# An encoder trunk on one core: tokens in column order for both mixers, and mixer B's probabilities turned in a band by 12 GpSimd copies in both layers

## The chip, the cores and the metric

One Trainium2 chip; the kernel runs on one of its NeuronCores. The engines that matter are TensorE (PE, with its weight loads shown apart as PEld), VectorE (DVE), ScalarE (ACT), GpSimd (POOL) and SyncE (SP), which here issues every DMA. The metric is the device time of one execution in microseconds (us), lower is better.

## The reference

Two layers, each a mixer sub-layer and a ConvFFN sub-layer, on 256 tokens of 2048 features; c is one conditioning vector. Cut to what matters:

```python
GRID_W, NA_KH, NA_KW, WIN = 64, 8, 16, 128     # SEQ 256: a grid of 4 rows of 64 tokens
for l in range(2):
    sh_a, sc_a, gt_a, sh_m, sc_m, gt_m = split(silu(c) @ ada_w[l] + ada_b[l], 6)
    h = rmsnorm(x, norm_mix[l]) * (1 + sc_a) + sh_a
    qa, ka, va, qb, kb, vb, ga, gb = split_cols(h @ w_in[l])
    ya = window_attention(rope(norm(qa)), rope(norm(ka)), va, sink_a[l]) @ w_proj_a[l]   # |i-j| <= 128, 8 heads
    yb = neighbourhood_attention(norm(qb), norm(kb), vb, rel_bias_b[l]) @ w_proj_b[l]    # 8 heads
    x = x + gt_a * ((sigmoid(ga) * ya + sigmoid(gb) * yb) @ w_out[l])
    h = rmsnorm(x, norm_ffn[l]) * (1 + sc_m) + sh_m
    g, v = split(depthwise_conv(h @ w_up[l], conv_w[l], conv_b[l]), 2)
    x = x + gt_m * ((silu(g) * v) @ w_down[l])
```

In mixer B a token sees the keys of all four grid rows in a window of 16 grid columns around its own column; the rest of a row of scores is masked.

## The kernel before

**Matrix work.** Activations lie with features on the 128 partitions and tokens along the free axis. Every float32 product with a big weight is made of three fp32r products of halves: weight and activation are each split into a rounded high part and the remainder (hi·hi, hi·lo, lo·hi). Weights stream from HBM in units of 16 blocks of 128x128 (1 MB, tile `w`); each half unit is cast on ACT into the high part of an `hl` tile (L326) and the remainder is made on DVE (L327). Four `hl` tiles and four raw tiles rotate, so a weight DMA, and behind it in SP's one queue all later DMAs, waits for a raw tile to come free. `feature_block` (L343 to L345) is the product for 128 output features of all 256 tokens; `tokens` (L406 to L408) is the q/k/v projection with tokens on the output partitions.

**Conditioning.** `ada` streams 96 tiles of 1 MB per layer (`aw`), each reduced by one DVE instruction (L233) into one column of `mod`; a plan by unit number says when.

**The mixer.** `normed` (L491 on) makes h: per 128 features a DVE instruction `ht` (L497), an ACT instruction (L500) and a DVE one (L501). The projection's groups of four heads pass through `qk_rows` (norms, rope, a turn to features on partitions) into the tiles `packA`, `packB`. Then heads run in a generator, `attention`: one call advances every live head by one stage and may start one more. Calls come from a pacer that ticks once per weight unit: 1.288 calls per tick in layer 0 until the last head of mixer A is done, then 0.36; 0.4 in layer 1. The stages of `attend` (L646 on) are:

1. scores on PE into PSUM `sc` (L651): one plain float32 product per 128 queries in layer 0 (two PE instructions each), three fp32r products in layer 1;
2. bias and row maximum on DVE (L654), exponent (L662) and scaling (L670) on ACT, in the tile `p`; in mixer B `p` holds the bias, loaded by a DMA, and then the scores;
3. the turn of the probabilities. In layer 0 four PE transposes per head into PSUM `tp` (L681). In layer 1 (`MOVED = [(0,0), (8,8)]`) one DVE transpose of 32x32 blocks into rows that are no longer needed (L304), then 16 GpSimd copies that put the blocks in place (L298), and one call of waiting;
4. the split into fp32r halves, `pT`, by an ACT cast (L418) and a DVE subtraction (L421); where the turn was made on DVE and GpSimd the cast is held in the program's order on ACT. `pT` has one buffer, so the next head's split waits until the products with v have read it;
5. six products with v (`po`, L689), and the output's split (L691, L692).

**The order of the work** on each engine comes from a list scheduler that runs when the program is built; an engine then takes its instructions strictly in that order, so a waiting instruction holds all that stands behind it. After the heads of layer 0 come: the projection of mixer A (`oA`, evacuated by `gated`, L434), the gate of mixer B, the merge (L1010 on: `gated` into a tile `m`, `ya` added in place (L1014), split), the output projection, the FFN.

**Constants.** `maskA` (256 KB) and the rope table `cs` are loaded by one DMA each, in `small` (L786 on) at the second of three passes over the q/k/v projection.

Of the kernel before, what the change touches and what calls it, by code (L numbers as in the profile page):

```python
# [15 lines left out]
P = 128  # L16
L = 2
D = 2048
S = 256
# [11 lines left out]
BLOCK = 32  # L31

# [57 lines left out]
MOVED = [(0,0), (8,8)]  # L90
# [51 lines left out]
def encoder(ctx: ExitStack, tc: tile.TileContext, a: dict, out: bass.AP):  # L142
# [45 lines left out]
    sp = pool("s", 1)  # L188

# [118 lines left out]

    def unit_steps(l, u, by_halves=False):
# [133 lines left out]
    class Squares:  # L443


        def __init__(self, name):
            self.acc = ev.tile([P, S], F32, name="sqa", tag="sqa", bufs=1)
            self.ps = ax.tile([P, 2, 2], F32, name=name, tag="ss", bufs=1)

        def add(self, mo):  # L450
            sq = self.acc if mo == 0 else ev.tile([P, S], F32, name="sq", tag="r", bufs=2)
            nc.scalar.activation(out=sq[:], in_=x[:, mo], func=AF.Square)
            if 0 < mo < KC - 1:
                nc.vector.tensor_tensor(out=self.acc[:], in0=self.acc[:], in1=sq[:], op=ALU.add)
            if mo == KC - 1:
                self.last = sq
# [34 lines left out]
    def normed(l, w, h, rbs):  # L491

        mod, amod = mods[l], amods[l]
        for kc in range(KC):
            t = ev.tile([P, S], F32, name="ht", tag="z")
            sh = mod[:, 3 * w * KC + kc : 3 * w * KC + kc + 1]
            nc.vector.scalar_tensor_tensor(  # L497
                out=t[:], in0=x[:, kc], scalar=amod[:, w, kc : kc + 1], in1=rbs[:], op0=ALU.mult, op1=ALU.mult
# [147 lines left out]
    def attend(q, k, v, p, mask, scale, sink, o, rows=None):  # L646

        sc = ax.tile([P, 2, S], F32, name="sc", tag="ax")
        for t in range(2):
            for i, j in by(q):  # L650
                nc.tensor.matmul(sc[:, t], q[i][:, t * P : (t + 1) * P], k[j], start=i + j == 0, stop=(i, j) == by(q)[-1])  # L651
        m = sm.tile([P, 2], F32, name="m", tag="m")
        for t in range(2):
            nc.vector.tensor_tensor_reduce(  # L654
                out=p[:, t], in0=sc[:, t], in1=mask[:, t], scale=scale, scalar=-3.0e38 if sink is None else sink,
                op0=ALU.add, op1=ALU.max, accum_out=m[:, t : t + 1],
            )
# [3 lines left out]
        for t in range(2):  # L661
            nc.scalar.activation(out=p[:, t], in_=p[:, t], func=AF.Exp, bias=nm[:, t : t + 1], accum_out=den[:, t : t + 1])  # L662
# [6 lines left out]
        for t in range(2):  # L669
            nc.scalar.activation(out=p[:, t], in_=p[:, t], func=AF.Copy, scale=ri[:, t : t + 1])  # L670
# [11 lines left out]
        pT = at.tile([P, 2, 2, S], F32R, name="pT", tag="pT", bufs=1)  # L682
        split(pT, tp[:], held=rows is not None)
# [101 lines left out]

    def small(l):  # L786

        if l == 0:
            tables.extend((load(a["maskA"], [P, 2, S], "maskA"), load(a["cs"], [P, 2, 2, HALF], "cs")))
# [18 lines left out]
    for l in range(L):  # L808
# [17 lines left out]
        if l:  # L826


            def bare_gate(mo):
                def evac(ps):  # L830
                    z, sh = bare.level(ps, 0.5)
                    half_tanh(ya[:, mo], z[:], bias=sh[:, :1])
# [17 lines left out]
        def head_a(i):  # L850
# [18 lines left out]
            def rows():  # L869
# [3 lines left out]
                q, k, v, p, tables[0], SCALE, sink[:, i : i + 1], lambda: oA[i], rows if i < MOVED[l][0] else None  # L873
            )

        def head_b(hb):
# [3 lines left out]
            nc.sync.dma_start(p[:], a["bias"][l, hb])  # L880
# [4 lines left out]
                q, k, lambda: in_halves(v[:, :, i * HEAD : (i + 1) * HEAD], f"vB{l}_{hb}", "vh", True), p, p, 1.0, None,  # L885
                lambda: oB_of(hb), (lambda: b[:, i : 9 + i : 8]) if hb < MOVED[l][1] else None,
            )

# [37 lines left out]
        for pi, (groups, gates) in enumerate(parts):  # L926
            last = pi == len(parts) - 1
            for g, part in enumerate(groups):
                have_h(part)
                pss = st.tokens(h, part)  # L930
                if pi == max(0, len(parts) - 2) and g == 0:
# [77 lines left out]
        for mo in range(KC):  # L1009

            def merge(ps):
                z = ev.tile([P, S], F32, name="m", tag="z")
                gated(z[:], gb[mo], ps)
                nc.vector.tensor_tensor(out=z[:], in0=z[:], in1=ya[:, mo], op=ALU.add)  # L1014
                split(merged[mo], z[:], 0.5)
# [188 lines left out]
```

## Time and profile before

| | us |
|---|---|
| median of 3 runs | 2655.18 (2653.85 to 2655.35) |
| the profiled execution: its own time | 2661.45 |
| its span in the trace | 2659.6 |
| PE busy (99%), weight loads busy (96%) | 2643.3, 2557.9 |
| DVE busy (80%) | 2121.0 |
| ACT busy (53%) | 1408.9 |
| GpSimd busy (9%) | 228.2 |

The granted TensorE clock is 1.00 throughout. The profiled execution lies 6.3 us above the median of the runs. A row of a group gives line, engine, operation, tile written <- tiles read, shapes and count, then busy time, the mean of one, and the idle time before them. A row by time gives start, duration, engine, line, and in brackets how long the engine was idle before it and on whom it waited. PE durations are latencies (about 277 ns for a 256-column product); the spacing of starts, about 113 to 117 ns, is what one costs in a stream.

### The profile page before, as it was taken

Reading aid. Unit: us, or ns where it says so; the run is one execution under the profiler, and the core shown is the slowest. Engines: PE = TensorE matmul, PEld = TensorE weight load, DVE = VectorE, ACT = ScalarE, POOL = GpSimd, SP = SyncE. Lnnn points to the kernel's source line nnn. Section 1 sums busy time; section 2 is a strip of 40 time slices with the busy share of each in tenths; the row PEclk is TensorE's granted clock in tenths of the full one; section 3 lists DMA queues with packets and bytes.
Section 4 is the critical chain, followed back from the end, with each engine's and each line's share of the span. In section 5 each row is a group of like instructions: output and inputs, shape, how many; then the busy total and the mean of one; then the engine's idle time right before and its main releaser. Section 6 shows DMA issues by size and latency. Waiting matters only on the chain.

```text
span 2659.6 us, 51014 instructions
## 1 busy us (share of the span) xinstructions
PE 2643.3 (99%) x21164; PEld 2557.9 (96%) x21164; DVE 2121.0 (80%) x2979; ACT 1408.9 (53%) x2280; POOL 228.2 (9%) x345
## 2 busy tenths in 40 slices
PE   9999999999999999999999999999999999999999
PEld 7888899999999999999998889999999999999999
DVE  8898998997987888788886778868888866655664
ACT  5445865456643555355554666654565445544553
POOL 0001100000000000000002558520000000000000
PEclk9999999999999999999999999999999999999999
DMA  9987779885777777877766666666747765555554
GB/s 371 349 329 292 267 294 356 316 339 184 295 272 289 284 287 285 306 296 285 283 221 253 249 234 232 253 258 257 283 178 287 297 252 191 192 196 194 196 191 143
DMA packets 102042, 700.42 MB, mean 263 GB/s; under 512 B 12721, under 2 KB 15025, under 8 KB 17969
## 3 DMA queue, kind: packets, MB, share of 16 engines
q1 hardware_dynamic: 101810, 697.17, 70.8%
q8 instruction: 165, 2.70, 0.4%
q14 instruction: 67, 0.55, 0.1%
HBM read 695.03 MB, written 2.10 MB: 262 GB/s over the span
## 4 chain that ended last, share of the span: by engine, by line
PE 86%; DMA 5%; DVE 5%; issue 2%; ACT 1%; POOL 0%; SPq 0%; DVEq 0%; ACTq 0%
PE ps L343 24%; PE ps L345 24%; PE ps L344 24%; DMA aw<-in_aw 4%; PE ps_t L408 4%; PE ps_t L407 4%; PE ps_t L406 4%; DVE hl L327 2%; DVE aw L233 1%; PE sc L651 1%; ACT hl L326 1%; PE po L689 1%; DMA w<-in_ws 1%; DVE u L1049 0%; POOL qrs L472 0%
## 5 line engine op out<-in xcount | busy, mean ns | idle before, releaser
L327 DVE TENSOR_TENSOR hl<-w,hl 128x1024 fp32r<-128x1024 f32 x928 | 1129.8, 1224 | 298.0 <-ACT hl L326 294.7
L326 ACT CAST hl<-w 128x1024 fp32r<-128x1024 f32 x928 | 969.8, 1049 | 719.7 <-PE ps L345 501.4
L343 PE MATMUL ps<-h,hl 128*128 128x256 f32 x3328 | 922.4, 277 | 1.3 <-DVE ya L970 0.6
L344 PE MATMUL ps<-h,hl 128*128 128x256 f32 x3328 | 919.6, 276 | 0.0
L345 PE MATMUL ps<-h,hl 128*128 128x256 f32 x3328 | 919.6, 277 | 0.0
L343 PEld LDWEIGHTS ps<-h,hl 128*128 128x128 f32 x3328 | 624.7, 188 | 2.4 <-DVE ya L970 0.8
L344 PEld LDWEIGHTS ps<-h,hl 128*128 128x128 f32 x3328 | 625.3, 188 | 0.4 <-DVE h L501 0.2
L345 PEld LDWEIGHTS ps<-h,hl 128*128 128x128 f32 x3328 | 624.4, 188 | 0.0
L233 DVE CUSTOM_DVE_ANT_0 aw<-aw,cact,ab 128x2048 f32<-128x2048 f32 x189 | 443.8, 2349 | 92.5 <-DMA aw<-in_aw 91.7
L406 PE MATMUL ps_t<-hl,h 128*128 128x512 f32 x576 | 223.0, 392 | 2.7 <-ACT h L500 2.0
L407 PE MATMUL ps_t<-hl,h 128*128 128x512 f32 x576 | 225.0, 391 | 0.3
L408 PE MATMUL ps_t<-hl,h 128*128 128x512 f32 x576 | 224.3, 390 | 0.0
L1049 DVE SCALAR_TENSOR_TENSOR u<-ps,cw,u 128x255 f32<-128x255 f32 x304 | 146.0, 480 | 62.0 <-ACT u L1047 58.1
L1047 ACT ACTIVATE u<-ps,cw 128x256 f32<-128x256 f32 x152 | 85.7, 564 | 155.4 <-PE ps L345 155.2
L343 PE MATMUL ps<-act_o,hl 128*128 128x256 f32 x512 | 142.0, 278 | 2.7 <-DVE u L1049 2.6
L345 PE MATMUL ps<-act_o,hl 128*128 128x256 f32 x512 | 142.1, 278 | 1.3 <-DVE hl L327 1.3
L344 PE MATMUL ps<-act_o,hl 128*128 128x256 f32 x512 | 142.0, 277 | 0.0
L345 PE MATMUL ps<-merged,hl 128*128 128x256 f32 x512 | 141.5, 277 | 0.0
L344 PE MATMUL ps<-merged,hl 128*128 128x256 f32 x512 | 141.5, 276 | 0.0
L343 PE MATMUL ps<-merged,hl 128*128 128x256 f32 x512 | 141.5, 277 | 0.0
L406 PEld LDWEIGHTS ps_t<-hl,h 128*128 128x128 f32 x576 | 107.9, 188 | 26.1 <-ACT h L500 3.0
L407 PEld LDWEIGHTS ps_t<-hl,h 128*128 128x128 f32 x576 | 108.1, 188 | 23.9 <-DVE hl L327 1.9
(244 smaller groups left out, 4800.3 us busy)
## 6 DMA issues: line engine op xcount, KB each, us to landing
w<-in_ws SPq DMA_DIRECT2D x463, 1024.0 KB, 4.9
aw<-in_aw SPq DMA_DIRECT2D x189, 1024.0 KB, 6.3
p<-in_bias SPq DMA_DIRECT2D x16, 256.0 KB, 4.5
x<-in_xT SPq DMA_DIRECT2D x4, 512.0 KB, 5.5
aw_o<-in_aw SPq DMA_DIRECT2D x2, 1024.0 KB, 12.4
out<-x SPq DMA_DIRECT2D x16, 128.0 KB, 3.2
w<-in_ws SPq DMA_DIRECT2D x2, 512.0 KB, 11.8
aw_b<-in_aw SPq DMA_DIRECT2D x1, 1024.0 KB, 18.1
```

What stands on the lines that cost most here:

```text
L233: nc.vector.tensor_tensor_reduce(out=raw[:], in0=raw[:], in1=cact[:], scale=1.0, scalar=ab[:, i : i + 1], op0=ALU.mult, op1=ALU.add, accum ...
L326: nc.scalar.copy(hl[:, 0], r)
L327: nc.vector.tensor_tensor(out=hl[:, 1], in0=r, in1=hl[:, 0].bitcast(F32), op=ALU.subtract)
L343: nc.tensor.matmul(out, hi, act[0], start=first, stop=False)
L344: nc.tensor.matmul(ps[:, :S], hi, act[1], start=False, stop=False)
L345: nc.tensor.matmul(out, lo, act[0], start=False, stop=last)
L406: nc.tensor.matmul(ps[:], xh, hi, start=kc == kcs[0], stop=False)
L407: nc.tensor.matmul(ps[:], xh, lo, start=False, stop=False)
L408: nc.tensor.matmul(ps[:], xl, hi, start=False, stop=kc == kcs[-1])
L651: nc.tensor.matmul(sc[:, t], q[i][:, t * P : (t + 1) * P], k[j], start=i + j == 0, stop=(i, j) == by(q)[-1])
L1047: nc.scalar.activation(out=u, in_=ps, func=AF.Identity, scale=w[:, 1:2], bias=w[:, 3:4])
L1049: nc.vector.scalar_tensor_tensor(out=u[:, to], in0=ps[:, of], scalar=w[:, j : j + 1], in1=u[:, to], op0=ALU.mult, op1=ALU.add)
```

## The change

**Token order.** A layer's mixer now works on tokens in column order: the four tokens of a grid column stand next to each other. `normed` writes `ht` in that order (runs of one element with a step of four), the bias, `maskA` and `cs` are loaded by `load_tokens` in 4 DMAs instead of 1 (8 for `cs`, whose two halves go apart), `maskA`'s columns are reordered by two GpSimd copies, the gate of layer 1 that is made from unnormalised x is written in the new order, and the merge writes the sum into a second tile, `m2`, back in the old order. `load_tables` is called in the first pass over the q/k/v projection, after its fourth group, ahead of where `small` loaded the tables.

**The band.** In column order 128 queries see 160 neighbouring keys (`NEAR`). For mixer B, in both layers, scores, mask, exponent, scaling and split work on 160 columns instead of 256, and the scores go into the two rows of q and k that the head has used up (`b[:, i:9+i:8]` of `packB`) instead of into `p`. The products with v keep 256 columns; the part of `pT` outside the band (two pieces of 96 columns per half) is set to zero once per layer by GpSimd.

**The turn.** `turned_near` takes the place of the four PE transposes in layer 0 and of DVE transpose and 16 copies in layer 1: a DVE transpose of the band into a tile of its own, `turned`, and 12 GpSimd copies back, 10 of 2x32 elements per partition on 32 partitions and 2 of 32. Its split is `split_near`, with the cast held on ACT. `MOVED = [0, 8]` keeps mixer A as it was: PE transposes in layer 0, DVE and 16 copies in layer 1. `WINDOWS_FROM = [0, 0]` turns all eight heads of mixer B in both layers.

**Tiles.** The two rotating square tiles of `Squares` (tag r) become one tile of the same total size, which `turned` shares by turns.

```diff
-MOVED = [(0,0), (8,8)]
+MOVED = [0, 8]
+WINDOWS_FROM = [0, 0]
...
+    def near(t):
+        return sheared(t, 0, S - NEAR, NEAR)
+    def load_tokens(dst, src):
+        rows = src.rearrange("(q w c) h f -> w q c h f", q=GRID_H // 2, w=2)
+        for w in range(2):
+            for q in range(GRID_H // 2):
+                nc.sync.dma_start(dst[q::2, w], rows[w, q])
...
+    def turned_near(p):
+        turned = ev.tile([P, 2, S], F32, name="turned", tag="r", bufs=1)[:]
+        nc.vector.transpose(out=near(turned), in_=near(p))
+        for a in range(P // BLOCK):
+            for d in (-1, 0, 1):
...
+                nc.gpsimd.tensor_copy(out=to, in_=of)
...
+    def split_near(dst, src, held):
+        high, low = near(dst[:, 0]), near(dst[:, 1])
+        copied = nc.scalar.copy(high, near(src))
+        if held:
+            tc.keep_in_program_order(copied)
+        nc.vector.tensor_tensor(out=low, in0=near(src), in1=high.bitcast(F32), op=ALU.subtract)
...
+            to, of, roots = (t[:], x[:, kc], rbs[:]) if w else (columns_by_row(t[:]), by_rows(x[:, kc]), by_rows(rbs[:]))
             nc.vector.scalar_tensor_tensor(
-                out=t[:], in0=x[:, kc], scalar=amod[:, w, kc : kc + 1], in1=rbs[:], op0=ALU.mult, op1=ALU.mult
+                out=to, in0=of, scalar=amod[:, w, kc : kc + 1], in1=roots, op0=ALU.mult, op1=ALU.mult
             )
...
-                nc.tensor.matmul(sc[:, t], q[i][:, t * P : (t + 1) * P], k[j], start=i + j == 0, stop=(i, j) == by(q)[-1])
+                nc.tensor.matmul(
+                    sc[:, t, :n], q[i][:, t * P : (t + 1) * P], k[j][:, part(t)], start=i + j == 0, stop=(i, j) == by(q)[-1]
+                )
...
+            to, of, add = p[:, t, part(t)], sc[:, t, :n], mask[:, t]
+            if window:
+                first = part(t).start // GRID_H
+                to, of = by_columns(to), by_columns(of)
+                add = rows_by_column(add)[:, first : first + n // GRID_H]
...
-            turned_blocks(p[:], rows(), 2)
-            for _ in range(STEPS[sink is None]):
+            if window:
+                turned_near(p)
+            else:
+                turned_blocks(p, rows(), 2)
+            for _ in range(STEPS[window]):
                 yield
...
-            tables.extend((load(a["maskA"], [P, 2, S], "maskA"), load(a["cs"], [P, 2, 2, HALF], "cs")))
+    def load_tables():
+        seen = at.tile([P, 2, S], F32, name="seen", tag="p")
+        load_tokens(seen[:], a["maskA"])
...
-            nc.sync.dma_start(p[:], a["bias"][l, hb])
+            load_tokens(p[:], a["bias"][l, hb])
...
-                nc.vector.tensor_tensor(out=z[:], in0=z[:], in1=ya[:, mo], op=ALU.add)
-                split(merged[mo], z[:], 0.5)
+                both = ev.tile([P, S], F32, name="m2", tag="z")
+                nc.vector.tensor_tensor(
+                    out=rows_by_column(both[:]), in0=by_columns(z[:]), in1=by_columns(ya[:, mo]), op=ALU.add
+                )
+                split(merged[mo], both[:], 0.5)
```

**How it moves instructions, at two places.** The first is the start of mixer B in layer 0, where the heads still come at 1.288 calls per tick. On DVE, from the second evacuation of mixer A's projection (`ya0`) on, before:

```order
L434 SCALAR_TENSOR_TENSOR ya0_222<-ya0_222,ps0_53_16_0_3417 128x256
L327 TENSOR_TENSOR hl0_54_0_3517<-w0_54_3515,hl0_54_0_3517 128x1024
L233 ISA aw0_45_3636,mod0_172<-aw0_45_3636,cact_100,ab0_173 128x2048
L233 ISA mod0_172 128x1
L421 TENSOR_TENSOR pT_3207<-tp_3202,pT_3207 128x512
L654 ISA p_3191,m_3216<-sc_3213,p_3191 128x256
```

and in the changed kernel at the same place (`packB0_0` holds the first head's probabilities, `hl0_54` and `hl0_55` are weight units):

```order
L377 TENSOR_TENSOR hl0_54_0_3558<-w0_54_3556,hl0_54_0_3558 128x1024
L347 STREAM_TRANSPOSE turned_3221<-packB0_0_224 128x2x160
L492 SCALAR_TENSOR_TENSOR ya0_222<-ya0_222,ps0_53_16_0_3446 128x256
L727 ISA packB0_0_224,m_3238<-sc_3235,p_3207 128x160
L727 ISA m_3238 128x1
L727 ISA packB0_0_224,m_3238<-sc_3235,p_3207 128x160
L727 ISA m_3238 128x1
L377 TENSOR_TENSOR hl0_54_1_3561<-w0_54_3556,hl0_54_1_3561 128x1024
L732 TENSOR_SCALAR nm_3241<-m_3238 128x2
L484 TENSOR_TENSOR pTB0_3324<-packB0_0_224,pTB0_3324 128x2x160
L492 SCALAR_TENSOR_TENSOR ya0_222<-ya0_222,ps0_54_8_0_3480 128x256
L377 TENSOR_TENSOR hl0_55_0_3621<-w0_55_3619,hl0_55_0_3621 128x1024
```

Between the transpose and the head's split (`pTB0`) now stand the second head's two mask instructions, half a weight unit and three short ones. The rest of unit 54 and unit 55 stand behind the split. On ACT the same head's cast is followed by the casts of the next units:

```order
L376 CAST hl0_54_1_3561<-w0_54_3556 128x1024
L685 ACTIVATE packB0_1_225<-qtp_3436,gains0_1005 128x4x128
L481 CAST pTB0_3324<-packB0_0_224 128x2x160
L376 CAST hl0_55_0_3621<-w0_55_3619 128x1024
L736 ACTIVATE packB0_0_224,den_3243<-packB0_0_224,nm_3241 128x160 x2
L376 CAST hl0_55_1_3624<-w0_55_3619 128x1024
```

so that a late copy holds back unit 55 on both engines.

The second place is SP's queue at the start. Before:

```order
L315 DMA w0_3_335<-in_ws 128x2048
L232 DMA aw0_7_371<-in_aw 128x2048
L315 DMA w0_4_383<-in_ws 128x2048
L232 DMA aw0_8_415<-in_aw 128x2048
L315 DMA w0_5_422<-in_ws 128x2048
```

and now:

```order
L365 DMA w0_3_335<-in_ws 128x2048
L223 DMA seen_349<-in_maskA 64x256 x4
L223 DMA cs_357<-in_cs 64x1x16 x8
L267 DMA aw0_7_388<-in_aw 128x2048
L365 DMA w0_4_400<-in_ws 128x2048
```

Twelve small DMAs moved ahead of the tile `aw0_7`; before, `maskA` and `cs` stood behind unit 15.

More of the change, by code (lines that the diff above doesn't have):

```diff
@@ L31 @@
 BLOCK = 32
+GRID_H = S // GRID_W
+NEAR = P + BLOCK
 QKV_GROUPS = [1024, 0, 512, 2560, 3584, 1536, 3072, 4096, 2048]
@@ L784, in encoder @@
     tables = []
+    def load_tables():
+        seen = at.tile([P, 2, S], F32, name="seen", tag="p")
+        load_tokens(seen[:], a["maskA"])
+        mask = const.tile([P, 2, S], F32, name="maskA")
+        for t in range(2):
+            nc.gpsimd.tensor_copy(out=by_columns(mask[:, t]), in_=rows_by_column(seen[:, t]))
+        cs = const.tile([P, 2, 2, HALF], F32, name="cs")
+        for f in range(2):
+            load_tokens(cs[:, f], a["cs"][:, f])
+        tables.extend((mask, cs))
     def small(l):
-        if l == 0:
-            tables.extend((load(a["maskA"], [P, 2, S], "maskA"), load(a["cs"], [P, 2, 2, HALF], "cs")))
         cs = tables[1]
```

66 lines of the change are left out of this document (53 added, 13 removed).

## The prediction

> **What bounds the kernel now.** I read the page's first lines and the chain that ended last, then the stretches which the change touches.
>
> ```profile
> span 2659.6 us, 51014 instructions
> PE 2643.3 (99%) x21164; PEld 2557.9 (96%) x21164; DVE 2121.0 (80%) x2979; ACT 1408.9 (53%) x2280; POOL 228.2 (9%) x345
> PE 86%; DMA 5%; DVE 5%; issue 2%; ACT 1%; POOL 0%; SPq 0%; DVEq 0%; ACTq 0%
> ```
>
> PE has work nearly all the time and carries 86% of the chain. What leaves PE's stream can therefore shorten the span, unless another engine stands right behind it. The view by stretches (per engine: busy time and instructions; then granted clock, DMA share, GB/s) says where one does: mixer B of layer 0 begins (340 to 376), goes on beside the projections (to 470), layer 0's merge (492 to 540), mixer B of layer 1 (1620 to 1680).
>
> ```profile
> 340.00:376.00 36.00, 36.00 (x288) 34.37 (x287) 34.45 (x69) 23.92 (x49) 0.00 (x0) 1.00 0.78 290
> 376.00:470.00 94.00, 94.00 (x813) 93.59 (x811) 85.09 (x118) 47.98 (x84) 0.00 (x0) 1.00 0.95 354
> 492.00:540.00 48.00, 48.00 (x422) 48.00 (x422) 47.49 (x81) 25.57 (x44) 0.00 (x0) 1.00 0.81 299
> 1620.00:1680.00 60.00, 60.00 (x529) 60.00 (x528) 51.32 (x78) 35.61 (x65) 48.48 (x78) 1.00 0.66 246
> ```
>
> In layer 0 PE and DVE are both full: DVE has 4% to spare at first, 1% in the merge, and from 376 on the DMAs are at 0.95. In layer 1 PE alone is full. So time taken from PE counts fully only while DVE is not made later.
>
> **What leaves PE.** The chain shows one head of mixer B in layer 0 (transposes, scores) and one head's scores in layer 1; the fourth row and its follower show products of one column.
>
> ```profile
> 375.79 0.44 PE tp L681 x4
> 376.23 0.86 PE sc L651 x4
> 1500.15 0.71 PE sc L651 x6
> 1934.65 0.50 PE L461 MATMUL ssm<-mean,sq 128*128 128x1 f32 x4
> 1935.01 0.36 PE L343 MATMUL ps<-bare_a,hl 128*128 128x258 f32 x1
> ```
>
> Transposes: 0.44 us a head, 8 heads, **-3.5 us**. Scores of layer 0: 0.86/4 = 215 ns an instruction at 256 columns; at 160 columns 134 ns in proportion. That is above the floor which the one-column products show (four start within 0.36 us, 90 ns each, with a weight load each), so 4 x 81 ns x 8 heads = **-2.6 us**. Together 6.1 us that PE certainly doesn't do.
>
> Scores of layer 1 are 48 fp32r products, 0.71/6 = 118 ns each at 256 columns. No fp32r product of fewer than 256 columns is in the trace. From below 90 ns bounds it (the one-column products): -1.3 us. From above the plain float32 rate, two instructions of 134 ns: 268 ns, +7.2 us. Nearest are fp32r products of 256 and 512 columns, whose cost goes with the columns, so I lean to the low end and take 105 ns: **-0.6 us**. The Trainium skill ("TensorE: Matmul & The Clock Gate", section "Back-to-back issue gap") gives N/2.4 + 2.5 ns for a warm product, whatever the type: 69 ns here by estimate, by which this term would be -2.4 us; the 90 ns of this trace speak against so much.
>
> **What is added.** Durations of what is done now:
>
> ```profile
> L654 DVE CUSTOM_DVE_ANT_0 p<-sc,p 128x256 f32<-128x256 f32 x32 | 12.3, 418 | 2.9 <-DMA p<-in_bias 2.7 <-PE sc L651 0.2
> L304 DVE STREAM_TRANSPOSE packB<-p 128x512 f32<-128x512 f32 x8 | 5.7, 709 | 5.1 <-ACT p L670 5.1
> L421 DVE TENSOR_TENSOR pT<-p,pT 128x512 fp32r<-128x512 f32 x16 | 11.9, 741 | 0.1
> L421 DVE TENSOR_TENSOR pT<-tp,pT 128x512 fp32r<-128x512 f32 x16 | 10.9, 683 | 0.8 <-ACT pT L418 0.8
> L298 POOL COPY p<-packB x128: 284/293/2415, 1641.5 to 1753.5; 32x128 f32<-32x128 f32 x128
> L298 POOL COPY packB<-qn x16: 392/398/1455, 1629.8 to 1641.0; 32x256 f32<-32x256 f32 x16
> 1668.44 8.76 POOL L298 COPY p<-packB 32x128 f32<-32x128 f32 x16 [4.82 <-issue]
> L1014 DVE TENSOR_TENSOR m<-m,ya 128x256 f32<-128x256 f32 x32 | 13.5, 421 | 0.3
> ```
>
> DVE grows by (741 - 418)/256 = about 1.05 us per 1000 elements and partition, between rows of different instructions. A head of layer 0 costs it 2 x 418 + 683 = 1519 ns now; then 2 x 317 for the mask, 509 for the transpose of 320 elements, 539 for the split: 1682 ns. That is 0.16 us a head, 1.3 us over 130 us in which DVE has 10 spare: nothing, if the waits below are left out. In layer 1 every step gets shorter on an engine that isn't the bound: nothing, and the same for ACT.
>
> A GpSimd copy takes 293 ns for 128 elements and 398 for 256 (medians), so about 188 + 0.82 per element: 240 ns for 64, 214 for 32; twelve take **2.8 us** undisturbed. The maximum of 2415 and the 8.76 us for 16 copies (4.7 by the median) say what DVE beside them does: 1.87 times as long, 5.2 us. Later heads come one per 13 to 18 us, which hides either.
>
> **The wait at the first heads.** Here the next call comes in the same or the next tick, so the split follows closely on the copies, and on ACT and DVE the casts of unit 55 are queued behind it. In the old kernel the first head went:
>
> ```profile
> 342.64 0.47 PE L345 MATMUL ps<-oA,hl 128*128 128x256 f32 x1
> 349.38 1.23 DVE L327 TENSOR_TENSOR hl<-w,hl 128x1024 fp32r<-128x1024 f32 x1
> 351.00 0.58 ACT L418 CAST pT<-tp 128x512 fp32r<-128x512 f32 x1
> 351.64 0.49 PE L689 MATMUL po<-pT,vB 128*128 128x256 f32 x2
> ```
>
> Scores done at 342.6, half unit 54 done on DVE at 350.5, cast at 351.0, products with v from 351.64. New: the transpose stands behind the same half unit, 350.3 to 350.8; twelve copies, with one half unit's DVE subtraction (1.1 us) in their way, to 354.7; cast to 355.1. PE has 61 weight products, 6 products with v, 4 score instructions and 8 transposes (0.86 us) queued between: 67 x 0.117 + 0.5 + 0.9 = 9.3 us, so it arrives at about 352.1 and waits **3.0 us**. The second head repeats it: transpose to 360, copies to 363.5, its cast holding ACT for about 4 us and its subtraction DVE for 2; the second half of unit 55 stands behind both and is ready at 366, when PE has wanted it since 363: **3.0 us**. A third wait at unit 57, behind the fourth head's exponent, I put at 1.5. Against these 7.5 us stand the waits that the old kernel has between the same points (about 2.2 us slower than its products' sum), and the PE time already saved there. Followed through to unit 57, PE is some 0.7 us earlier than before, where 3.4 would have been due: **+2.7 us** given back. What is late next is unit 57 and the products with v of the second head, which the slower pace then covers. Of the 2.7 still to be saved on heads five to eight I count 1.9, as DMAs at 0.95 can't follow at once: **+0.8 us**.
>
> **The start.** `maskA` and `cs` go ahead of `aw0_7`.
>
> ```profile
> 29.24 0.33 SPq L315 DMA_DIRECT2D w<-in_ws  x1
> 33.78 0.33 SPq L232 DMA_DIRECT2D aw<-in_aw  x1
> 96.52 0.43 SPq L178 DMA_DIRECT2D maskA<-in_maskA  x1
> 96.99 0.43 SPq L178 DMA_DIRECT2D cs<-in_cs  x1
> 33.98 0.50 DVE ht L497
> 42.80 2.34 DVE L233 CUSTOM_DVE_ANT_0 aw<-aw,cact,ab 128x2048 f32<-128x2048 f32 x1
> aw<-in_aw SPq DMA_DIRECT2D x189, 1024.0 KB, 6.3
> ```
>
> Twelve issues of 0.44 us from 29.6 end at 34.9, 1.1 us after `aw0_7` could go. It lands 6.3 later, at 41.2, before DVE takes it at 42.8: covered. Without that cover it would cost up to 1.1, and the 288 KB another 0.8 in a stretch full of DMAs. Two GpSimd copies of 256 elements (0.4 each or more) may hold DVE once. I take **+0.3**, from 0 to 2. The 48 extra bias issues (1.3 us of SP per head) lie beside transfers already queued: nothing, at most 1. The second tile in the merge, the zeroing once per layer and the new home of the squares: nothing; the three tiles that rotate there are each read within one 2.7 us product.
>
> **Steps of one element.** `ht` (16 in the start of layer 0, on the chain at 33.98), the mask (steps of 64 in the bias) and the merge's sum (steps of 64 in its output) now move element by element at a stride; no row shows such a DVE operation. From below it costs nothing more; from above I let every element cost a second 1.05 ns: 0.27 us for 256 elements. I take nothing, because the trace shows the same 1.05 ns per element whether an operand comes from SBUF or from PSUM, and none of its rows is slower by its pattern. The Trainium skill ("SBUF — State Buffer", section "Door 1: The DMA port swizzle") speaks against it: runs should hit a 16-byte line at least twice, and each new line costs. By that rule the second rival holds; no run here shows it yet.
>
> **Sum.** -6.1 + 2.7 + 0.8 - 0.6 + 0.3 = **-2.9 us** on the profiled execution: 2661.45 would become 2658.6. That execution is 6.3 above the median of the runs, so the median goes from 2655.2 to **2652.3**.
>
> **Rivals.**
> - *Narrow fp32r products run at the plain float32 rate.* For it: the only narrow products in the trace are plain ones. Price (268 - 105) x 48 = 7.8 us on PE in layer 1, where nothing hides it: **2660.1**, slower than before. It turns the sign from (0.105 x 48 + 2.9)/48 = 165 ns a product on.
> - *Strided DVE operations cost a second pass.* 5 of the `ht` lie on the chain (1.3), the merge of layer 0 has 1% of DVE to spare (16 x 0.27 = 4.3, most of it shows), the mask adds 0.17 x 16 where DVE waits anyway (1): some 6 us, **2658.5**. Both together: 2666.
> - *The waits are longer:* copies take 5.2 us beside DVE, three times 1.5 more: **2657**.
> - *The waits don't reach PE*, since weight units lie further ahead than I count: all 6.1 and the floor of layer 1 come in, **2648.5**.
> - *It saves PE's time but DVE or the DMAs are the bound of layer 0,* so nothing moves: **2655**.
>
> **How the numbers follow.** Forecast 0.38 (own range 2649.5 to 2656), narrow products 0.22, strides 0.15, both 0.05, longer waits 0.08, no waits 0.07, nothing moves 0.05. A run of this kernel can tell about 0.2%, 5.3 us, from no change: below 2649.9 lie the no-wait case and a tail of the forecast (0.14), above 2660.5 about half of the narrow products, both together and tails of strides and waits (0.28). The range is 2648 to 2663.
>
> **What would show it.** Right: `tp` gone in mixer B and `sc` of four instructions at 0.54 us; a gap on PE ahead of the first `po` with `pTB` of about 3 us, and a second one at a weight unit some 10 us later, with GpSimd's copies the releaser; then no PE wait from 380 on. In layer 1 six `sc` in about 0.63 us; at 1.6 us the first rival holds. `ht` and the merge's sum at 477 and 421 ns, or at 740 and 690 for the second. Wrong altogether: PE idle in the merge or in layer 1's heads, or SP late with weights at 40 to 90.

## The result, and the profile after

The changed kernel takes **2671.1 us** (median of 6 runs, 2666.7 to 2672.8) beside 2654.5 for the kernel before (6 runs): ratio 1.0053, 95% interval 1.0042 to 1.0065. So it is **about 14 us slower** by the ratio, 16.6 by the medians. Forecast were 2652.3 and a range that ended at 2663.

The page's first lines and the chain of the changed kernel:

```profile
span 2671.0 us, 51124 instructions
PE 2642.6 (99%) x21132; PEld 2556.3 (96%) x21132; DVE 2124.8 (80%) x2987; ACT 1399.5 (52%) x2280; POOL 252.8 (9%) x415
PE 76%; DVE 10%; DMA 8%; issue 3%; ACT 2%; POOL 1%; DVEq 0%; ACTq 0%; POOLq 0%; SPq 0%
```

PE carries 76% of the chain in place of 86; DVE and the DMAs took over the rest. PE's own work did get shorter: it has 32 instructions fewer, and in layer 0 the instructions of a narrow score mostly start 135 ns apart, those of a full one 218. So it waits. To see where, take the same weight product in both traces (both have 20,544 products with `hl`, in the same order) and subtract its start before from its start now. I call this the lag; every table below uses it.

| product | us before | lag after | what lies between |
|---|---|---|---|
| 49 | 36.0 | +0.5 | |
| 121 | 53.8 | +6.5 | `maskA` and `cs` are loaded |
| 1561 | 322.9 | +6.4 | other layer-0 work: nothing |
| 2473 | 452.6 | +12.2 | heads of mixer B, layer 0 |
| 4801 | 724.3 | +14.2 | merge (500 to 610 us) and output |
| 11001, 12501 | 1480, 1734 | +11.4, +11.5 | heads of mixer B, layer 1: nothing |

So 14.2 us are lost by 724 us: **6.4 at the start, 5.8 at the heads, 2.0 after them.** Later lags mislead, because the profiled execution of before loses time of its own:

```profile
782.41 0.36 PE L343 MATMUL ps<-act_o,hl 128*128 128x256 f32 x1 [2.62 <-DVE u L1049]
```

PE waits there, and its products then start 118 ns apart, not 113, until 867: together 6.0 us. Another 1.9 go between 1264 and 1340. No other profile of this study loses as much at the first place (h2_p3 has half of it) or any of the second, and together they account for that execution lying 6.3 above its median. The changed kernel's profile in turn loses 4.7 us between 1264 and 1310, behind late `aw` transfers, which no other profile shows.

**The start.** SP's row of the changed kernel from 29.5 on (start, us, line, transfer, count), what SP waited for between 26 and 42, one stretch of the kernel before, three of the changed one, and DVE's row behind them:

```profile
29.54 0.33 SPq L365 DMA_DIRECT2D w<-in_ws  x1
29.92 2.47 SPq L223 DMA_DIRECT2D seen<-in_maskA  x4
32.43 8.82 SPq L223 DMA_DIRECT2D cs<-in_cs  x8
41.36 0.53 SPq L267 DMA_DIRECT2D aw<-in_aw  x1
```

```profile
SPq L223 <- DMA w<-in_ws: 2.0, 1, 2.0
SPq L223 <- DMA aw<-in_aw: 1.9, 1, 1.9
```

```profile
34.00:43.00 9.00, 8.24 (x35) 6.13 (x34) 7.97 (x9) 6.54 (x9) 0.00 (x0) 1.00 0.91 362
```

```profile
34.00:43.00 9.00, 8.21 (x34) 5.83 (x32) 7.91 (x11) 6.30 (x9) 3.31 (x2) 1.00 0.47 142
43.00:51.00 8.00, 4.01 (x17) 2.93 (x16) 4.02 (x6) 0.23 (x1) 0.00 (x0) 1.00 0.94 390
51.00:56.00 5.00, 4.04 (x11) 3.26 (x12) 3.98 (x5) 3.81 (x6) 0.00 (x0) 0.66 0.94 388
```

```profile
48.11 2.35 DVE L268 CUSTOM_DVE_ANT_0 aw<-aw,cact,ab 128x2048 f32<-128x2048 f32 x1 [3.90 <-DMA aw<-in_aw]
```

`aw0_7` goes at 41.36, not 33.78. Twelve issues took 11.3 us, not 5.3: an issue costs 0.6 us, not 0.44, and twice SP stood for 2 us. The instruction records say why. Each DMA adds to one of eight landing counters, taken in turn, and SP issues it only when the DMA that used this counter last has landed. The third and fourth `cs` are the eighth after `aw0_6` and `w0_3`, and go 0.02 us after these have landed (35.61 and 38.14). Meanwhile the DMA engines run dry: 0.47 of their time and 142 GB/s, where the old kernel has 0.91 and 362. DVE then waits 3.9 us for `aw0_7`, PE is busy for half of 43 to 51, and afterwards has a lower clock (0.66 over 5 us).

**The heads.** GpSimd's twelve copies for each of the eight heads, and PE at the first of them:

```profile
357.22 4.08 POOL L357 COPY packB<-turned 32x32 f32<-32x32 f32 x12 [5.33 <-DVE turned L347]
366.88 3.29 POOL L357 COPY packB<-turned 32x32 f32<-32x32 f32 x12 [5.58 <-DVE turned L347]
375.86 5.15 POOL L357 COPY packB<-turned 32x32 f32<-32x32 f32 x12 [5.70 <-DVE turned L347]
382.88 6.35 POOL L357 COPY packB<-turned 32x32 f32<-32x32 f32 x12 [1.86 <-PE sc L717]
395.81 6.90 POOL L357 COPY packB<-turned 32x32 f32<-32x32 f32 x12 [6.58 <-DVE turned L347]
414.15 5.21 POOL L357 COPY packB<-turned 32x32 f32<-32x32 f32 x12 [11.44 <-DVE turned L347]
420.99 11.23 POOL L357 COPY packB<-turned 32x32 f32<-32x32 f32 x12 [1.64 <-DVE turned L347]
436.19 11.18 POOL L357 COPY packB<-turned 32x32 f32<-32x32 f32 x12 [3.97 <-DVE turned L347]
361.84 0.50 PE L772 MATMUL po<-pTB,vB 128*128 128x256 f32 x2 [2.42 <-ACT pTB L481]
```

The copies take 3.3 to 11.2 us; forecast were 2.8, or 5.2 at worst. (The median of a copy is 232 ns, near the 240 forecast; the mean is 520.) The wait before the first `po` is there, on the cast that is held behind the copies, as forecast. Then stretches of before, and of the changed kernel:

```profile
340.00:360.00 20.00, 20.00 (x155) 18.89 (x154) 18.79 (x40) 12.75 (x27) 0.00 (x0) 1.00 0.77 280
360.00:380.00 20.00, 20.00 (x165) 19.38 (x164) 19.66 (x41) 12.45 (x26) 0.00 (x0) 1.00 0.80 304
```

```profile
340.00:360.00 20.00, 19.22 (x155) 18.41 (x153) 18.59 (x41) 12.22 (x30) 2.94 (x10) 1.00 0.59 202
360.00:380.00 20.00, 18.16 (x143) 18.16 (x144) 15.13 (x31) 9.03 (x24) 7.76 (x26) 0.91 0.53 189
380.00:400.00 20.00, 17.61 (x149) 17.15 (x148) 16.85 (x29) 9.16 (x19) 10.60 (x26) 1.00 0.90 356
```

From 340 to 380, where the old kernel moves 280 to 304 GB/s, this one moves 189 to 202. The weights that weren't moved there are missing from 385 on: PE is busy for 17.6 of 20 us, with the transfers back at 0.90. The forecast "no PE wait from 380 on" is wrong.

**The merge and `ht`.** Rows of the changed kernel: `ht`, the merge's sum, the mask, and the scores of both layers:

```profile
L557 DVE SCALAR_TENSOR_TENSOR ht<-x,amod,rbs 128x256 f32<-128x256 f32 x64 | 34.4, 576 | 0.5
L1120 DVE TENSOR_TENSOR m<-m,ya 128x256 f32<-128x256 f32 x32 | 20.2, 631 | 0.2
L727 DVE CUSTOM_DVE_ANT_1 packB<-sc,p 128x160 f32<-128x160 f32 x32 | 12.9, 435 | 0.9 <-PE sc L717 0.8
L717 PE MATMUL sc<-packB 128*128 128x160 f32 x32 | 6.8, 321 | 0.0
L717 PE MATMUL sc<-kB,qB 128*128 128x160 f32 x48 | 6.4, 269 | 0.0
```

The sum takes 631 ns (421 before). The 32 `ht` with a stride take (64 x 576 - 32 x 477)/32 = 675 (477). The mask takes 435 on 160 elements, where 317 were expected. That is 0.2 us for 256 elements, so the second rival's mechanism is real.

### The profile page after: what moved, and what is told of

It is laid out like the page before. It is cut to its first block, busy times and chain, and to the rows that moved or that the text cites. A ratio compares the mean times of both kernels' runs of the same rounds, so it can differ in the third digit from the quotient of the medians.

```text
span 2671.0 us, 51124 instructions
## 1 busy us (share of the span) xinstructions
PE 2642.6 (99%) x21132; PEld 2556.3 (96%) x21132; DVE 2124.8 (80%) x2987; ACT 1399.5 (52%) x2280; POOL 252.8 (9%) x415
## 4 chain that ended last, share of the span: by engine, by line
PE 76%; DVE 10%; DMA 8%; issue 3%; ACT 2%; POOL 1%; DVEq 0%; ACTq 0%; POOLq 0%; SPq 0%
PE ps L393 21%; PE ps L395 21%; PE ps L394 21%; DMA aw<-in_aw 8%; PE ps_t L456 4%; PE ps_t L458 4%; PE ps_t L457 4%; DVE hl L377 4%; DVE aw L268 3%; ACT hl L376 1%; PE sc L717 1%; PE po L772 1%; DVE u L1157 0%; POOL qrs L531 0%; ACT qsq L638 0%
## 6 DMA issues: line engine op xcount, KB each, us to landing
aw_b<-in_aw SPq DMA_DIRECT2D x1, 1024.0 KB, 18.3
```

## The experiments

Theory A: the loss is made in the queue of transfers. SP issues in order, and short DMAs take places there and hold back the weights. Theory B: it is made on the engines, by DVE's strided steps and by GpSimd's copies with what is held behind them. Both were tested place by place, because each of them may hold at one place only.

Times are medians; the ratio is to the kernel before, run on the same chip with it. That kernel's own median was 2654.5 beside the change, 2655.6 beside the e runs, 2654.3 beside the f runs and 2654.8 beside the g and h runs, so a difference between runs of two letters is uncertain by a microsecond more. Three places are read from each trace: the lag at product 1561 (start, and whatever else comes before the heads), what the heads add (to 2473), and what is added by 4801.

| run | us | ratio, 95% interval | start | heads | to 724 us |
|---|---|---|---|---|---|
| the change | 2671.1 | 1.0053 (1.0042 to 1.0065) | +6.4 | +5.8 | +2.0 |
| e1_late | 2670.2 | 1.0061 (1.0048 to 1.0074) | +8.0 | +6.5 | +0.6 |
| e2_onedma | 2657.2 | 1.0004 (0.9995 to 1.0013) | +2.5 | -1.6 | +3.1 |
| e3_w8 | 2664.4 | 1.0032 (1.0019 to 1.0045) | +4.8 | -0.4 | +3.6 |
| e4_plain | 2666.1 | 1.0042 (1.0029 to 1.0055) | +3.6 | +5.6 | +0.4 |
| f1_two | 2660.6 | 1.0013 (0.9989 to 1.0036) | +2.1 | +0.7 | +5.8 |
| f2_pool | 2670.8 | 1.0062 (1.0050 to 1.0075) | +3.5 | +2.0 | +4.0 |
| f3_onedma_plain | 2653.5 | 0.9997 (0.9988 to 1.0006) | +1.8 | -1.2 | +0.7 |
| f5_before4 | 2660.8 | 1.0022 (1.0013 to 1.0032) | +6.1 | -0.2 | +1.2 |
| g1_pe_less | 2648.6 | 0.9975 (0.9965 to 0.9984) | 0.0 | -6.2 | +2.0 |
| g2_p3 | 2668.8 | 1.0056 (1.0044 to 1.0068) | +4.8 | +4.0 | +2.1 |
| g3_strides | 2658.3 | 1.0015 (1.0007 to 1.0024) | +1.5 | +0.3 | +1.2 |
| g4_plain_w8 | 2653.8 | 0.9996 (0.9987 to 1.0005) | +1.7 | -2.5 | +0.5 |
| h2_p3 | 2667.3 | 1.0042 (1.0029 to 1.0055) | +5.3 | +4.8 | +2.6 |
| h3_rows4 | 2679.4 | 1.0091 (1.0078 to 1.0104) | +5.0 | +19.4 | +2.5 |

Each lag is one execution, and the same order of work gives lags that differ by up to 1.6 us (the start is the same in the change, e3, g2, h2 and h3: 4.8 to 6.4).

**e1_late.** The tables go back to where they were loaded before.

```diff
-                if l == 0 and pi == 0 and g == 3:
-                    load_tables()
...
+        if l == 0:
+            load_tables()
         cs = tables[1]
```

> The 12 short DMAs of maskA and cs go back to the place behind unit 15. The changed kernel is 6.5 us behind the old one at 100 us of the span (same weight product). Theory A (SP issues in order, and a DMA waits until the one that used its landing semaphore eight DMAs earlier has landed, so that 12 short ones hold back the next weights while the DMA engines run empty): the lag at 100 us falls to 0.5 to 1, the DMA share between 36 and 42 us goes back over 0.9, and the time falls by 5 to 7 us. Theory B (the loss at the start is DVE's: the two GpSimd copies of maskA and the strided ht slow it): the lag stays above 4, since ht keeps its stride. If later waits for DMAs hide the gain, the lag at 100 us falls and the time does not.

The lag at 100 us fell to 1.5, near what theory A has, and the DMA share between 36 and 42 us is 0.73 (0.20 in the change, 0.84 before). At the old place the lag then rose from 1.5 (product 481) to 8.0 (product 1201), and the time stayed. The place wasn't the trouble: twelve short DMAs cost as much at either place.

**e2_onedma.** One DMA for each load.

```diff
-        for w in range(2):
-            for q in range(GRID_H // 2):
-                nc.sync.dma_start(dst[q::2, w], rows[w, q])
+        nc.sync.dma_start(dst, src)
```

> Each table and each bias is loaded with one DMA in place of four (maskA 1, cs 2, bias 1; the same bytes, with the tokens in row order, so that another attention is computed). Places stay as in the change. Theory A by the count of DMAs: the lag at 100 us falls from 6.5 to 1 or 2, and of the 5.8 us that are lost between 340 and 470 us at least 3 go too; the time falls by 8 to 11. Theory A by the place alone (a bias DMA that waits for its buffer p holds back the weights behind it, whether one or four): the start is mended, 340 to 470 is not; the time falls by 5 to 6. Theory B (DVE and GpSimd): nothing changes by more than 1 us.

About 14 us came back, more than either form of theory A gave, at both places (start +2.5, heads -1.6). The same two stretches in this run:

```profile
340.00:360.00 20.00, 17.58 (x145) 17.13 (x144) 16.89 (x39) 12.06 (x30) 4.08 (x14) 1.00 0.86 309
360.00:380.00 20.00, 19.20 (x166) 19.00 (x166) 16.74 (x34) 11.70 (x26) 10.91 (x26) 1.00 0.67 242
```

The copies and the first head's wait are still there (PE 17.6 of 20), yet the transfers run at 309 and 242 GB/s, and the wait is made up for.

**e3_w8.** `WINDOWS_FROM = [8, 0]`: TensorE turns layer 0's heads again.

> The heads of mixer B in layer 0 are turned by TensorE transposes again (the narrow band and everything else stay as in the change). Theory B (the turn by GpSimd copies, with the cast held on ACT behind it, makes PE wait and holds p longer): the loss between 340 and 470 us falls from 5.8 to 1 or less, PE has no wait of more than 1 us there beyond the waits of the kernel before, and the time falls by 4 to 6. Theory A by the count (four bias DMAs a head): at least 3 of the 5.8 stay. The start keeps its 6.5 in both.

The loss at the heads went (-0.4), with four DMAs for a bias still there. So neither the DMAs nor the copies make it alone.

**e4_plain.** The three strided steps follow the rows.

```diff
-            to, of, roots = (t[:], x[:, kc], rbs[:]) if w else (columns_by_row(t[:]), by_rows(x[:, kc]), by_rows(rbs[:]))
+            to, of, roots = (t[:], x[:, kc], rbs[:])
...
-                    out=rows_by_column(both[:]), in0=by_columns(z[:]), in1=by_columns(ya[:, mo]), op=ALU.add
+                    out=both[:], in0=z[:], in1=ya[:, mo], op=ALU.add
```

> The three steps of DVE that go element by element at a stride (ht, the mask, the merge's sum) go along the rows instead; tokens are then mixed up, so another function is computed. ht falls from 0.68 to 0.48 us, the merge's sum from 0.63 to 0.42, the mask from 0.43 to 0.32. If the strides cost time: the start gains 0.5 to 1 us, the stretch from 500 to 740 the 2 us that it lost, the time falls by 2 to 4. If DVE hides them, the lag changes by less than 1 at every place.

5.0 us by the medians, 2.9 by the ratios: the merge's loss went almost wholly (0.4), part of the start's too, nothing at the heads (5.6). Not all of the start's gain is the strides': the change has half the clock for 3.4 us at 51.6, which can cost it 1.7, and this execution has none there.

**f1_two.** `maskA` and each bias in two DMAs of 128 rows, `cs` from GpSimd's queue.

```diff
-        rows = src.rearrange("(q w c) h f -> w q c h f", q=GRID_H // 2, w=2)
+        rows = src.rearrange("(q w c) h f -> w c h q f", q=GRID_H // 2, w=2)
         for w in range(2):
-            for q in range(GRID_H // 2):
-                nc.sync.dma_start(dst[q::2, w], rows[w, q])
+            nc.sync.dma_start(dst[:, w], rows[w])
```

> maskA and each bias in two DMAs of 128 rows in place of four of 64 rows (tokens by columns as in the change), cs's eight from GpSimd's queue, so that SP issues 2 DMAs for a head and 2 at the start. Theory A by the count: a loss between those of one and of four DMAs; the lag at 100 us is 1.5 to 2.5, of the 5.8 us between 340 and 470 about 2 stay; the time is 2658 to 2662. Theory B (GpSimd's copies with what stands behind them on ACT and DVE, which one DMA a head hid by another order of the instructions): the 5.8 stay, 2664 or more.

As theory A has it, between one and four: the heads add -1.6, +0.7 and +5.8 us with one, two and four DMAs. After the heads it loses 5.8, more than any other run, and why isn't seen. It is the fastest form of the change found that still computes the reference; it beats the change, not the kernel before.

**f2_pool.** `nc.gpsimd.dma_start` in `load_tokens`, nothing else.

> All short DMAs of maskA, cs and bias (4, 8 and 4 a head as in the change) are issued by GpSimd, so that SP's queue holds the weights alone. Theory A, if what counts is SP's order (weights behind a bias that waits for its buffer, and 0.6 us for each issue): the start loses 2 us or less, 340 to 470 no more than 1; 2655 to 2658. Theory A, if what counts is the number of transfers, wherever they are issued: as in the change, 2668 or more. GpSimd has its copies between these issues; a bias that comes late by that would show as DVE waiting for it, and 2660 to 2665.

It came out as in the change, but not for the reason given there: start and heads lose less (+3.5, +2.0), and 9.3 us are lost in layer 1, between products 11001 and 12001 (PE's wait, and half the clock for 6.8 us around it). What DVE and PE wait for there:

```profile
DVE packB L727 <- DMA p<-in_bias: 8.9, 2, 8.3
```

```profile
PE ps L393 <- ACT hl L376: 5.4, 1, 5.4
```

The bias stands behind GpSimd's copies, and the mask waits 8.3 us for it. The order of a queue counts, whichever engine has it.

**f3_onedma_plain.** e2_onedma and e4_plain together.

> One DMA for each table and bias, and the three strided DVE steps along the rows (two runs of before in one; tokens are in row order, another attention is computed). What is left of the change is the turn by GpSimd and the narrow band. If the strides' cost adds to that of the DMAs: 2 to 4 us below the run with one DMA alone, 2653 to 2655, and 2652.3 if the rest of the forecast held. If DVE's strides only showed where DMAs were late: 2657 as without this.

2653.5: the strides cost 3.7 us here by the medians (e2 took 2657.2), 1.9 by the ratios. What is left of the change is as fast as the kernel before.

**f5_before4.** The kernel before with its loads cut as in the change.

```diff
+    def in_pieces(dst, src):
+        for w in range(2):
+            for q in range(2):
+                nc.sync.dma_start(dst[q::2, w], src[q::2, w])
...
-            nc.sync.dma_start(p[:], a["bias"][l, hb])
+            in_pieces(p[:], a["bias"][l, hb])
```

> The kernel before, with nothing changed but that maskA and each bias are loaded in four DMAs of 64 rows and cs in eight, in the same places and in the same order of tokens. Theory A by the count alone: it loses 6.5 us where the tables are loaded (as the run with late tables did between 105 and 232 us) and 4 to 6 at the heads of mixer B, together 8 to 12: 2663 to 2667. If the heads' loss needs GpSimd's copies too: 6 to 7, 2661 to 2662. If the count costs nothing: 2655.

6 us, all of it at the tables (lag 0.6 at product 481, 6.1 at 1201); the heads lose nothing. The middle case, as with e3.

**g1_pe_less.** The kernel before, with PE's saving and nothing added.

```diff
+        less = sink is None and rows is None
+        cols = [slice(96 * t, 96 * t + 160) if less else slice(0, S) for t in range(2)]
...
+        elif less:
+            tp = p
```

> The kernel before, with the prediction's 6.1 us taken from PE in layer 0 and nothing put in their place: mixer B's heads there compute 160 of 256 columns of scores and split p itself in place of its transpose (32 transposes left out, so that another function is computed). If PE bounds layer 0, as the prediction took it: 2649 (6 below before). If the transfers bound it from 376 us on (share 0.95), as the run with one DMA and plain strides suggests, whose heads gave 1.3 of the 6.1: no more than 1 to 2 us, 2653 to 2654, and the lead at 470 us is 2 or less.

2648.6, 6.2 below before: I had come to doubt the first term of the forecast, and it holds to 0.1 us. PE bounds layer 0, not the transfers; my second theory of f3's small gain falls.

**g2_p3 and h2_p3.** A third buffer for `p`; h2 keeps GpSimd's source in a place of its own.

```diff
-            p = at.tile([P, 2, S], F32, name="p", tag="p")
+            p = at.tile([P, 2, S], F32, name="p", tag="p", bufs=3)
```

> The changed kernel with a third buffer for p, so that a bias DMA need not wait for the head two before it (room for it: the source of GpSimd's copies goes into the buffer of the normalized queries, the squares into p's). Four DMAs for a bias as in the change, the start as in the change. Theory A (weights stand behind a bias that waits for its buffer; at 371 to 377 us nothing is in flight): of the 5.8 us between 340 and 470 at least 3 go, the DMA share between 360 and 380 rises from 0.5 to over 0.7; 2665 to 2668. Theory B (GpSimd's copies with what is queued behind them): the 5.8 stay, 2670 to 2672. The start's 6.5 stay in both.

> The changed kernel with a third buffer for p; room for it comes from a source for GpSimd's copies of 320 elements in place of 512, in the buffer of the spread roots, which is free then, and from squares of q and k that nobody reads, kept in 16 bits. Four DMAs for a bias, start as in the change. If SP's wait for p, with the weights behind it, makes the heads' loss: at most 2 of the 5.8 us stay, the DMA share between 360 and 380 is over 0.75, the time 2664 to 2667. If GpSimd's copies and the casts held behind them make it: 4 or more stay, 2669 to 2671.

The heads add 4.0 and 4.8: neither half nor nothing for g2, and for h2 the case "4 or more stay". In h2 SP's idle time ahead of bias DMAs fell from 29 us to 10 between 340 and 470 us, and the DMA share between 360 and 380 rose from 0.53 to 0.76, as the first case has it, and yet most of the loss stayed. So the wait for `p` is at most a small part. SP's idle time ahead of weight units rose instead, from 38 us to 56.

**g3_strides.** The kernel before with `ht` and the merge's sum written at a stride (the edits of e4, the other way round).

> The kernel before, with nothing changed but that ht (16 in each layer) and the merge's sum are written element by element at a stride, as in the change (tokens get mixed up, so another function is computed). If the strides' price holds without the rest (0.2 us each, on a DVE that is full in the merge and in the start): +0.8 at the start, +2 to +3 in the merge of layer 0, nothing in layer 1, where DVE has room; 2657 to 2658. If the loss between one DMA with and without strides came from the mask or from the order of instructions: 2655.

3.4 us by the medians, near what f3 won by leaving them out. In this execution 1.5 show at the start and 1.2 in the merge, the one more and the other less than I expected.

**g4_plain_w8.** f3 with `WINDOWS_FROM = [8, 0]`.

> One DMA for each table and bias, steps along the rows, and layer 0's heads turned by TensorE (as in the kernel before); of the change only the narrow band and the heads of layer 1 are left. If the turn by GpSimd is worth something once DMAs and strides are out of the way, this is 1 to 3 us slower than the run that has it (2653.5). If the transfers bound these heads anyway: the same within 1 us, with the first head's wait of 4 us gone and nothing more at 470 us.

Equal to f3 within 0.3 us. Here the narrow scores alone give 2.5 at the heads, near the 2.6 forecast. The turn by GpSimd, which takes 3.5 from PE, adds nothing on balance: its waits cost as much in the time, and at the heads 1.3 us more.

**h3_rows4.** Four DMAs of 32 whole rows for each bias.

```diff
-            load_tokens(p[:], a["bias"][l, hb])
+            for r in range(0, P, P // 4):
+                nc.sync.dma_start(p[r : r + P // 4], a["bias"][l, hb][r : r + P // 4])
```

> The changed kernel with each bias in four DMAs of 32 whole rows (2 KB a row; tokens in row order, so another attention is computed) in place of 64 halves of rows (1 KB). If SP's time for the issues counts (0.6 us each, 2.4 a head): an issue takes about 0.35, and half or more of the 5.8 us go, 2665 to 2668. If the number of DMAs and their place ahead of the weights count, whatever an issue takes: 4 or more of the 5.8 stay, 2669 to 2671.

Worse than either case, though an issue takes 0.42 us in place of 0.6. SP's order is another one here:

```profile
341.38 7.99 SPq L974 DMA_DIRECT2D p<-in_bias  x8
349.48 0.36 SPq L365 DMA_DIRECT2D w<-in_ws  x1
351.89 7.35 SPq L974 DMA_DIRECT2D p<-in_bias  x8
359.29 0.42 SPq L267 DMA_DIRECT2D aw<-in_aw  x1
366.02 1.70 SPq L974 DMA_DIRECT2D p<-in_bias  x4
367.77 0.42 SPq L365 DMA_DIRECT2D w<-in_ws  x1
```

Sixteen bias DMAs with one weight unit among them, and 18.3 us from that unit to the next; the largest such gap is 14.9 in the change, 13.0 in e2 and 10.0 before. The gap alone doesn't tell, though: h2 has one of 19.8 and loses 4.8, e3 one of 14.2 and loses nothing.

**What stays open at the heads.** MB moved in the first 45 us from product 1633 on, beside what the heads add:

| | g1 | g4 | before | f5 | f3 | e3 | e2 | f1 | h2 | e4 | change | h3 |
|---|---|---|---|---|---|---|---|---|---|---|---|---|
| MB | 14.6 | 14.2 | 13.6 | 12.8 | 12.7 | 12.6 | 12.6 | 12.0 | 11.9 | 11.0 | 10.9 | 9.9 |
| us | -6.2 | -2.5 | 0 | -0.2 | -1.2 | -0.4 | -1.6 | +0.7 | +4.8 | +5.6 | +5.8 | +19.4 |

Reckon from g4, which has the narrow band and neither copies nor short DMAs in layer 0's heads. The copies alone (f3) cost 1.5 MB and 1.3 us more than TensorE's turn, the four DMAs alone (e3, which has the strides too) 1.6 MB and 2.1 us, both together (e4) 3.2 MB and 8.1 us. The bytes add up and the time doesn't: together they cost 4.7 us more than the two added, where a lag is uncertain by 1 to 2.

The traces show where the time goes. From product 1561 to 1901 (380 us before) the change gains 0.8 us and f3 0.9: the first head's wait is in both, and both make up for it. By product 1951 the change has lost 2.1, f3 has still gained 0.2. In between the change's PE waits for one weight unit, 0.63 us for its cast (below) and then 1.75 for its remainder:

```profile
376.79 2.99 SPq L223 DMA_DIRECT2D p<-in_bias  x4
380.51 0.38 SPq L365 DMA_DIRECT2D w<-in_ws  x1
387.82 1.99 ACT L376 CAST hl<-w 128x1024 fp32r<-128x1024 f32 x2 [4.23 <-DMA w<-in_ws]
388.92 0.39 PE L393 MATMUL ps<-oA,hl 128*128 128x256 f32 x1 [0.63 <-ACT hl L376]
```

SP issues this unit behind four bias DMAs, at 380.51; in f3 it goes at 371.01. So at this place the loss reaches PE as a weight unit that SP asked for late. Which of SP's steps makes it late isn't shown: ACT's and DVE's instructions come in another order in f3 and e2 than in the change from 374 us on at the latest, a late PE also frees buffers late, and a run with the same order and fewer transfers wasn't made.

## Why the prediction was wrong, step by step

| step | forecast | measured | by |
|---|---|---|---|
| what leaves PE in layer 0 | -6.1 | -6.2 | g1 |
| waits and later limits at the heads | +2.7 + 0.8 | +5.0 | heads of f3 less those of g1 |
| narrow scores, layer 1 | -0.6 | about 0 | lag 11.4 and 11.5 on both sides |
| the start | +0.3 | +6.4 | lag; 12 DMAs cost 6.5 in e1, 5.6 in f5; with one DMA a load 1.8 to 2.5 stay (f3, e2) |
| 48 more bias issues | 0, at most 1 | +7.3, +6.8 | heads of the change less those of e2, of e4 less those of f3 |
| strided steps | 0 | about +2 to +5 | g3, f3, e4 |

The rows overlap (part of the strides' price falls in the start), so they don't add up exactly to what the change lost.

Two steps failed by their mechanism, and they cost most. **"Twelve issues of 0.44 us from 29.6 end at 34.9 ... covered"**: I counted SP's time for an issue and took it from DMAs of another shape. I didn't ask what a DMA must wait for before it can be issued, and so missed the landing counters: twelve short transfers put SP behind 1 MB transfers still under way. **"The 48 extra bias issues lie beside transfers already queued: nothing, at most 1"**: with one DMA a load and the steps along the rows (f3) 0.8 us are won of the 2.9 forecast, which is no change clear of noise; with four DMAs the heads alone lose about 7 more. I had seen that the DMAs can't catch up at 0.95, and used it for 0.8 us of PE's gain only, not for bytes asked for late.

**"I take nothing" for strides** was a wrong choice between two stated ends: 0.2 us an operation, near the upper 0.27. (The slope behind it is misreckoned: (741 - 418)/256 is 1.26 ns an element, not 1.05. The durations worked out with 1.05 came out all the same: 0.51 us for the transpose, and 317 ns for the mask once its strides are gone, in e4.) The Trainium skill's rule cited there ("SBUF — State Buffer", section "Door 1: The DMA port swizzle") speaks for the upper end, and the rows agree with it: 0.8 ns more for each element.

Right were the first term and the first head's wait (PE waits 2.4 us for `pTB`; forecast 3.0). The second and third waits, 3.0 and 1.5 us at units 55 and 57, didn't come there: PE next waits at 388.92, for the late unit shown above. Six narrow scores of layer 1 on the chain of the changed kernel:

```profile
1634.39 0.64 PE sc L717 x6
```

0.64 us, where full ones took 0.71: the first rival (1.6 us) was false. But most of them start 112 ns apart, nearly at the pace of full ones (113). Only the first is followed after 71 ns, the weight products behind them give that back (one starts 155 ns after the other, not 113 to 120), and the lag shows no gain. The 69 ns that the prediction worked out from the Trainium skill ("TensorE: Matmul & The Clock Gate", section "Back-to-back issue gap") are far from this; the section gives that formula for an isolated product and says that it counts too little at small N, where the weight load is left out. The waits and later limits at the heads in layer 0 were put 1.5 us too low. The copies take up to 11 us, and half the clock behind the first wait can cost 1.7; how much is due to either isn't shown.

Of the rivals none was the case. The second (strides) holds as a mechanism, with about 2 to 5 of its 6 us; the longer waits hold in part. The largest cost, short DMAs in a full queue, wasn't among them.

## What to carry to other kernels

When a change splits a load, count the queue's places, not the bytes: see in the trace how many DMAs may be under way, and what large transfer the next one must wait for. Ask the same of whatever stands behind it on that queue. And when several small losses fall into one stretch with the transfers at 0.95, don't add them: two that cost 1.3 and 2.1 us alone cost 8.1 together here.

## What the hardware showed that I had not expected

SP needs 0.33 us to issue a DMA of 128 rows of 8 KB or of 2 KB, 0.42 for 32 rows of 2 KB, and 0.6 for 64 rows, on every other partition, of 1 KB or 64 bytes. The bytes don't decide it: 64 KB take 0.42 us in 32 rows and 0.6 in 64.

A wait of PE can cost more than its length. Two stretches of the changed kernel around the first `po`:

```profile
358.00:362.00 4.00, 1.58 (x14) 1.38 (x13) 1.62 (x5) 0.82 (x3) 2.95 (x9) 1.00 0.31 107
362.00:366.00 4.00, 4.00 (x21) 4.00 (x22) 3.87 (x5) 3.72 (x10) 0.00 (x0) 0.57 0.79 284
```

PE stood for 2.4 of the 4 us up to 362, and the clock granted in the next 4 us was 0.57 (half of it for 3.4 us, by the clock records). The Trainium skill ("TensorE: Matmul & The Clock Gate", section "What's actually happening") puts the half clock behind an idle window of about 3.4 us; here a shorter wait brought it. It doesn't always: the first `po` is late by 2.4 us in e1, e2, e4, f1, f3 and h2 too, and half the clock follows in e4, f1, f3 and h2, but not in e1 and e2, nor behind the 2.62 us at 782 of the kernel before.
